# A two-layer decoder trunk on one core: the FFN output product of 22 row tiles, 14 of them as seven products of half blocks

## The chip, the cores and the metric

The kernel runs on one core of a Trainium2 chip. A core has a matrix engine (TensorE, in profiles PE for matmuls and PEld for loading their stationary operand), VectorE (DVE), ScalarE (ACT), GpSimd (POOL) and SyncE (SP, which here only issues DMAs). The metric is the device time of one execution in microseconds (us). Before the change the median of three runs is 1255.21 us (1253.51 to 1259.88).

## The reference

Two layers work on 512 tokens of 1024 features, in float32. Layer 0 mixes tokens with a convolution module, layer 1 with native sparse attention (NSA); after each mixer comes the same dense network (FFN) with its own weights. The inner width D_FF is 2816.

```python
for i in range(DEPTH):                       # DEPTH = 2
    h = rmsnorm(x, norm_mix[i])
    y = conformer_conv_module(h, ...) if i == 0 else nsa_attention(h, positions, ...)
    x = x + y
    h = rmsnorm(x, norm_ffn[i])
    x = x + swiglu_ffn(h, ffn_w_in[i], ffn_w_out[i])

def swiglu_ffn(h, w_in, w_out):
    gate, up = jnp.split(h @ w_in, 2, axis=-1)
    return (jax.nn.silu(gate) * up) @ w_out      # (512 x 2816) @ (2816 x 1024)
```

## The kernel before

All activations are kept transposed: x is eight tiles x[m] of 128 features by 512 tokens. Products run in float32 precision by splitting: each float32 operand is written as a high part (rounded to the fast format fp32r, by ScalarE) and a low part (the rest, by VectorE), and a block product is three matmuls: high x high, low x high and high x low. In the names, `wh` and `wl` are the two parts of weights, `ah` and `al` those of the FFN's inner activations y, `hh` and `hl` those of the normalized input.

**Weights.** A planned list `units` gives the order of all weight tiles of 128 x 1024 floats. SyncE loads them into a ring of three buffers `wr` (`w_dma`, line 188); `w_hi` (ScalarE, line 198) and `w_lo` (VectorE, line 207) split them into rings `wh` and `wl` of two buffers each. `next_w` takes the next unit, issues its split and loads ahead.

**Inner part of the FFN.** The 22 row tiles of gate and up are 5 plain ones and 17 "pairs". A pair replaces the eight half-block products of a 2 x 2 scheme by seven (Strassen's way), on sums of weights and of activations: 84 matmuls with 256 columns (`product`, line 840). The weight sums of a pair come from GpSimd: `s_pre` loads a tile S (line 803), `s_acc` adds a second block to it by an accumulating DMA (line 807), and `s_add` forms two further sums (lines 814 and 815). They are split like weights (`s_part`, lines 823 and 824).

**Output part.** For each output tile m the 22 row tiles are used plainly, in units of 8, 8 and 6 blocks: a block is three matmuls of 512 columns (`mm3`, lines 258 to 260), so a layer has 22 x 8 x 3 = 528. `OUT_ORDER` interleaves the first two m, since the activations are only just being made. When a tile m is complete, VectorE adds it to x (line 985) and, in layer 0, `finish_x` prepares the next stage: the split of x (ScalarE, and VectorE in line 293) and the sum of its squares (`sum_x`: the addition in line 302 is GpSimd's for all tiles but the last, by `fin`). The same happens at the end of the convolution module and of NSA. In layer 1 the result is stored instead, the last tile in two halves of 256 columns.

**Rope tables.** `rope_tables` (lines 995 to 1018) computes sine and cosine tables for NSA, thirteen operations on VectorE and three on ScalarE, and is called within layer 0's output part.

**Order.** Within the inner part and the output part most instructions are kept in the order in which the program writes them on each engine (`pe`, `held`, `parted`); elsewhere a scheduler chooses.

Of the kernel before, what the change touches and what calls it, by code (L numbers as in the profile page):

```python
# [91 lines left out]
OUT_ORDER = [(m, b) for b in range(3) for m in range(2)] + [(m, b) for m in range(2, NK) for b in range(3)]  # L92
OUT_N = 256
# [15 lines left out]
def trunk(ctx: ExitStack, tc: tile.TileContext, A, out):  # L109
# [27 lines left out]

    def add_ffn(l):
# [5 lines left out]
        for m, b in OUT_ORDER:  # L144
            add("fw_o8", l * 16 + m * 2 + b, 1024) if b < 2 else add("fw_o6", l * 8 + m, 768)
# [37 lines left out]
    def w_dma(i):  # L183
        if i in raws or i >= len(units):
            return
        ap, cols = units[i]
        t = wp.tile([P, 1024], F32, tag="wr", name=f"wr{i}")
        raw_dma[i] = after(nc.sync.dma_start(t[:, :cols], ap), state.get("behind"))
        raws[i] = t
# [98 lines left out]
    def split_x(m, gcol):  # L288
# [3 lines left out]
        nc.scalar.activation(hh[m], x[m], AF.Copy, scale=g)  # L292
        nc.vector.scalar_tensor_tensor(hl[m], x[m], g, hh[m], ALU.mult, ALU.subtract)

    def sum_x(m, acc, eng=None, on_v=False):
        sq = acc if m == 0 else tp.tile([P, T], F32, tag="sq", name=nm("sq"))
        if on_v:
            nc.vector.tensor_tensor(sq, x[m], x[m], ALU.mult)
        else:
            nc.scalar.activation(sq, x[m], AF.Square)  # L300
        if m > 0:
            (eng or nc.gpsimd).tensor_tensor(acc, acc, sq, ALU.add)  # L302
# [4 lines left out]

    def fin(m):
        return nc.vector if m == NK - 1 else nc.gpsimd
# [57 lines left out]
    def proj_tile(pool, tag, xh=None, xl=None, mid=None, fixed=False):  # L367
# [16 lines left out]
        return ps  # L384


    def conv_module():
        acc = new_acc()
        with ExitStack() as cx:
# [307 lines left out]
            acc = new_acc()  # L697
            for m in range(NK):
# [6 lines left out]
    def ffn(acc, gnext, layer, between=None):  # L705
# [9 lines left out]
        with ExitStack() as cx:  # L715
# [3 lines left out]
            pa = cx.enter_context(tc.tile_pool(name="fpa", bufs=2, space=PSUM, reuse_waits="tile"))  # L719
            sx = ExitStack()  # L720
# [78 lines left out]

            def s_pre(n):  # L800
                if n < NST:
                    S[n] = sw.tile([P, 2 * T], F32, tag="S", bufs=3, name=nm("S"))
                    pe(nc.gpsimd.dma_start(S[n], fw_x(n)[:, :2 * T]))

            def s_acc(n):
                if n < NST:
                    pe(nc.gpsimd.dma_start(S[n].rearrange("p (a b) -> p a b", a=2),  # L807
                                           fw_x(n)[:, None, 2 * T:].to_broadcast([P, 2, T]), accum_op=ALU.add))

# [57 lines left out]
            def pair(n, prev):  # L867
# [6 lines left out]
                s_g2(n)  # L874
                s_acc(n + 2)
                s_add(n + 1)
# [55 lines left out]
            pss, w, ws = {0: bank()}, {0: next_w(False)}, {}  # L932

            def out_mm(m, fs):
                wh, wl = w[m]
                for f in fs:
                    c = slice(f % 8 * P, (f % 8 + 1) * P)
                    mm3(pss[m], wh[:, c], wl[:, c], ah[f], al[f], f == 0, f == NF - 1)

            def parts(*fs):  # L940
                for f in fs:
                    divide(f, fo)

            hold[0] = True
            out_mm(0, range(4))
            w_hi(state["next"])
            w_lo()
# [4 lines left out]
            parts(4, 5, 6, 7)  # L952
            pss[1] = bank()
            w[1] = next_w(False)
            out_mm(1, range(4))
            out_mm(0, range(4, 8))
            parts(8, 9, 10, 11)
            w_hi(state["next"])
            w_lo()
            out_mm(1, range(4, 8))  # L960
            parts(12, 13, 14, 15)
            w[0] = next_w(False)
            w_hi(state["next"])
            out_mm(0, range(8, 16))
            w_lo()
            parts(16, 17, 18)
            w[1] = next_w(False)
            w_hi(state["next"])
            out_mm(1, range(8, 16))
            w_lo()  # L970
            parts(19, 20, 21)
            hold[0] = False
            acc = new_acc() if gnext is not None else None
            for m, b in OUT_ORDER[4:]:
                if m not in pss:
                    pss[m] = bank()
                ps = pss[m]
                w[m] = next_w()
                if (m, b) == (3, 0) and layer == 0:
                    between()  # L980
                out_mm(m, range(8 * b, min(8 * b + 8, NF)))
                if b < 2:
                    continue
                if gnext is not None:
                    nc.vector.tensor_tensor(x[m], x[m], ps, ALU.add)
                    finish_x(m, gnext, acc, fin(m))
                else:
                    n = OUT_N if m == NK - 1 else T
                    for c in range(0, T, n):
                        nc.vector.tensor_tensor(x[m][:, c:c + n], x[m][:, c:c + n], ps[:, c:c + n], ALU.add)  # L990
                        nc.sync.dma_start(out[m][:, c:c + n], x[m][:, c:c + n])
# [3 lines left out]
    def rope_tables():  # L995
        rp = hx[0].enter_context(tc.tile_pool(name="rp", bufs=1))
        cosT = rp.tile([P, T], F32, name="cosT")
        sinT = rp.tile([P, T], F32, name="sinT")
        pos = tp.tile([P, T], I32, tag="sq", name="pos")
# [834 lines left out]
```

## Time and profile before

| | |
|---|---|
| median of three runs | 1255.21 us (1253.51 to 1259.88) |
| the profiled execution | 1256.96 us, span 1255.2 us, granted TensorE clock 0.995 |
| TensorE matmuls | 8015 recorded, busy 98% of the span |
| VectorE, ScalarE, GpSimd | busy 66%, 45% and 27% |
| DMA | 161.62 MB moved, 129 GB/s in the mean |
| output part of a layer | 422.7 to 547.8 us (layer 0), 1125.9 to about 1251 us (layer 1) |

The span is the time from the first to the last instruction on the profiled core; the rest of an execution lies around it. A busy share is a mean over all stages. A matmul's printed duration is longer than the distance to the next one's start, because matmuls overlap in the pipeline; what a stream costs is read from the starts. Lines "L258" name lines of the kernel.

### The profile page before, as it was taken

Reading aid. Unit: us, or ns where it says so; the run is one execution under the profiler, and the core shown is the slowest. Engines: PE = TensorE matmul, PEld = TensorE weight load, DVE = VectorE, ACT = ScalarE, POOL = GpSimd, SP = SyncE. Lnnn points to the kernel's source line nnn. Section 1 sums busy time; section 2 is a strip of 40 time slices with the busy share of each in tenths; the row PEclk is TensorE's granted clock in tenths of the full one; section 3 lists DMA queues with packets and bytes.
Section 4 is the critical chain, followed back from the end, with each engine's and each line's share of the span. In section 5 each row is a group of like instructions: output and inputs, shape, how many; then the busy total and the mean of one; then the engine's idle time right before and its main releaser. Section 6 shows DMA issues by size and latency. Waiting matters only on the chain.

```text
span 1255.2 us, 20744 instructions
## 1 busy us (share of the span) xinstructions
PE 1226.4 (98%) x8015; PEld 1036.0 (83%) x8015; DVE 827.4 (66%) x1455; ACT 566.0 (45%) x1046; POOL 340.8 (27%) x395
## 2 busy tenths in 40 slices
PE   9999899999999999999998999999999999999998
PEld 6787788799999988887777776667878999998886
DVE  6995587788888735336697777753497766656221
ACT  5221464445554533223453677773354555544111
POOL 2010021144444001132332465651303444410000
PEclk9999999999999999999998999999999999999999
DMA  8757636457766233253166011001624877722331
GB/s 304 267 133 270 170 101 185 118 148 180 185 177 161 60 110 99 93 151 112 60 150 162 18 25 36 1 18 52 197 88 112 205 192 188 181 82 97 110 112 43
DMA packets 82115, 161.62 MB, mean 129 GB/s; under 512 B 36064, under 2 KB 36960, under 8 KB 80480
## 3 DMA queue, kind: packets, MB, share of 16 engines
q1 hardware_dynamic: 65808, 108.54, 28.3%
q0 software_dynamic: 16208, 51.75, 16.2%
q8 instruction: 63, 1.03, 0.3%
q14 instruction: 36, 0.29, 0.1%
HBM read 146.73 MB, written 5.28 MB: 121 GB/s over the span
## 4 chain that ended last, share of the span: by engine, by line
PE 72%; DVE 9%; issue 9%; POOL 5%; ACT 3%; DMA 1%; SPq 1%; DVEq 0%; POOLq 0%; ACTq 0%
PE st L840 17%; PE pp L258 7%; PE pp L260 7%; PE pp L259 7%; PE st L260 7%; PE st L258 7%; PE st L259 7%; PE O L1576 3%; PE cpe L496 2%; POOL S L815 1%; POOL S L814 1%; PE T L1550 1%; DVE Pm L1522 1%; PE S L1519 1%; POOL S L807 1%
## 5 line engine op out<-in xcount | busy, mean ns | idle before, releaser
L198 ACT ACTIVATE wh<-wr 128x1024 fp32r<-128x1024 f32 (+3 forms) x158 | 160.4, 1015 | 299.1 <-PE st L259 143.3
L207 DVE TENSOR_TENSOR wl<-wr,wh 128x1024 fp32r<-128x1024 f32 (+3 forms) x158 | 191.0, 1209 | 123.6 <-ACT wh L198 123.2
L840 PE MATMUL st<-bh,sh 128*128 128x256 f32 x680 | 194.1, 285 | 0.7 <-DVE t L865 0.7
L840 PE MATMUL st<-bh,sl 128*128 128x256 f32 x680 | 192.5, 283 | 1.1 <-DVE sl L824 1.1
L840 PE MATMUL st<-bl,sh 128*128 128x256 f32 x680 | 192.0, 282 | 0.0
L258 PE MATMUL pp<-hh,wh 128*128 128x512 f32 x400 | 158.8, 399 | 2.6 <-ACT wh L198 2.4
L260 PE MATMUL pp<-hh,wl 128*128 128x512 f32 x400 | 157.4, 396 | 1.7 <-DVE wl L207 1.7
L259 PE MATMUL pp<-hl,wh 128*128 128x512 f32 x400 | 157.9, 396 | 0.0
L824 DVE TENSOR_TENSOR sl<-S,sh 128x512 fp32r<-128x512 f32 x136 | 117.4, 899 | 46.9 <-ACT sh L823 45.4
L260 PE MATMUL st<-ah,wl 128*128 128x512 f32 x352 | 139.6, 396 | 0.0
L258 PE MATMUL st<-ah,wh 128*128 128x512 f32 x352 | 139.5, 396 | 0.0
L259 PE MATMUL st<-al,wh 128*128 128x512 f32 x352 | 139.5, 396 | 0.0
L840 PEld LDWEIGHTS st<-bh,sh 128*128 128x128 f32 x680 | 129.9, 191 | 2.5 <-DVE t L865 1.1
L840 PEld LDWEIGHTS st<-bh,sl 128*128 128x128 f32 x680 | 130.1, 191 | 1.5 <-DVE sl L824 1.5
L840 PEld LDWEIGHTS st<-bl,sh 128*128 128x128 f32 x680 | 130.5, 192 | 0.1
L1537 POOL TENSOR_SCALAR Pm<-Pm,sm,gates 128x512 f32<-128x512 f32 (+3 forms) x128 | 79.8, 636 | 64.9 <-DVE sm L1533 52.2
L258 PEld LDWEIGHTS pp<-hh,wh 128*128 128x128 f32 x400 | 75.3, 188 | 23.9 <-ACT wh L198 5.0
L302 POOL TENSOR_TENSOR acc<-acc,sq 128x512 f32<-128x512 f32 x18 | 30.9, 1718 | 226.8 <-ACT sq L300 208.9
L260 PEld LDWEIGHTS pp<-hh,wl 128*128 128x128 f32 x400 | 75.2, 188 | 20.4 <-DVE wl L207 3.3
L814 POOL TENSOR_TENSOR S<-S,wr 128x512 f32<-128x512 f32 x34 | 53.9, 1586 | 135.1 <-DMA wr<-fw_in 72.9
L259 PEld LDWEIGHTS pp<-hl,wh 128*128 128x128 f32 x400 | 75.4, 188 | 18.2 <-issue 1.1
L1523 ACT ACTIVATE Pm<-Pm,mx 128x512 f32<-128x512 f32 (+3 forms) x128 | 71.0, 557 | 37.7 <-DVE mx L1522 33.2
(292 smaller groups left out, 2556.1 us busy)
## 6 DMA issues: line engine op xcount, KB each, us to landing
S<-fw_x POOLq DMA_DIRECT2D x68, 512.0 KB, 6.0
wr<-fw_in SPq DMA_DIRECT2D x46, 512.0 KB
wr<-fw_o SPq DMA_DIRECT2D x32, 512.0 KB
bd<-bands POOLq DMA_DIRECT2D x12, 1280.0 KB, 12.3
r<-fw_x SPq DMA_DIRECT2D x34, 256.0 KB
wr<-cw_in SPq DMA_DIRECT2D x14, 512.0 KB
wr<-fw_o SPq DMA_DIRECT2D x16, 384.0 KB
wr<-fw_s SPq DMA_DIRECT2D x8, 512.0 KB
```

The lines of the kernel that those rows point to most:

```text
L198: parted(after(nc.scalar.activation(hi[:, :cols], raws[i][:, :cols], AF.Copy), pin.get(AF)))
L207: parted(after(nc.vector.tensor_tensor(lo[:, :cols], raws[i][:, :cols], hi[:, :cols], ALU.subtract), pin.get(ALU)))
L258: held(nc.tensor.matmul(ps, wh, xh, start=first, stop=False))
L259: held(nc.tensor.matmul(ps, wh, xl, start=False, stop=False))
L260: held(nc.tensor.matmul(ps, wl, xh, start=False, stop=last))
L302: (eng or nc.gpsimd).tensor_tensor(acc, acc, sq, ALU.add)
L814: pe(nc.gpsimd.tensor_tensor(t[:, :T], S[n][:, :T], w[:, :T], ALU.add))
L824: pe(nc.vector.tensor_tensor(l_[:, c], z, h_[:, c], ALU.subtract))
L840: pe(nc.tensor.matmul(ps[:, :H], p_[:, k], m_[c][:, t], start=first and c == 0 and q == 0, stop=last and c == 3 and q == 2, skip_group_che ...
L1523: at_[AF] = nc.scalar.activation(Pt, Pt, AF.Exp, bias=mx, scale=-1.0, accum_out=sm)
L1537: nc.gpsimd.tensor_scalar(Pt, Pt, sm[:, k:k + 1], gates[:, t + k, br * 16 + h:br * 16 + h + 1], ALU.mult, ALU.mult)
L1576: pe(nc.tensor.matmul(o[par * 64:par * 64 + 64, P * kc:], vf[br][:, kc, g], Us[par][kc], start=False, stop=last))
```

## The change

The output part uses the first 8 row tiles (EARLY + LATE) plainly, as before, in eight units `PLAIN` of eight blocks. The other 14 are taken as 2 halves of NO = 7 row tiles; together with 2 halves of the outputs (m 0 to 3 and 4 to 7) and 2 halves of the tokens they form a 2 x 2 scheme whose eight products are replaced by seven, numbered p = 1 to 7 and done in the order `OUT_SEQ`. Each has 28 blocks (4 outputs x 7 row tiles) of three matmuls with 256 columns: 84 matmuls, in units (p, u) of 8, 8, 8 and 4 blocks. The plain units stand between them as slots P1 to P7 (`PLAIN_AT`). In layer terms 528 matmuls of 512 columns become 192 of 512 and 588 of 256; PE's instruction list grows by 504 rows.

For p = 1, 4 and 7 the weights are quarters of the matrix that come through the `wr` ring. For p = 2, 3, 5 and 6 they are sums: SyncE loads a quarter (`s_base`), GpSimd adds others by accumulating DMAs (`s_more`). One sum tile per unit is kept and carried on from product 2 to 3 to 5; the first one lies in the three S buffers of the inner part (pool `so`), the sum for p = 6 (`S6`) has its own buffers and is begun in product 4. Sums are split into the same `wh` and `wl` rings (`split_sum`). Activations need sums and differences too (`z_new`, `z_on`, on VectorE), split by `direct` and `summed`. Results of a product collect in PSUM and are added to x by `out_add`, in halves of 256 columns.

In each slot the program writes, in this order: the split of the next slot's weights, this slot's matmuls, the additions to x of the previous slot's results, and what `todo` lists for this slot.

Further edits: in a pair GpSimd's `s_add` for the next pair now stands ahead of `s_acc`; the sums of squares of the convolution's, layer 0's and NSA's outputs are added on VectorE throughout; the rope tables are computed in the convolution's output part, written to DRAM and reloaded in NSA; layer 1's last tile adds and stores one half at the end.

```diff
-OUT_ORDER = [(m, b) for b in range(3) for m in range(2)] + [(m, b) for m in range(2, NK) for b in range(3)]
+LATE = 4
+NO = (NF - EARLY - LATE) // 2
+QCOLS = 4 * NO * P
+QU = (QCOLS + 1023) // 1024
+OUT_SEQ = (1, 4, 2, 3, 5, 6, 7)
+OUT_RAW = {1: 0, 4: 1, 7: 3}
+OUT_SUMS = ((2, 3, (2,)), (3, 3, (2, 0)), (5, 3, (2, 0, 1)), (6, 0, (2,)))
...
+PLAIN_AT = {(4, 1): 3, (2, 2): 4, (3, 0): 5, (5, 0): 6, (5, 2): 7}
...
-    def fin(m):
-        return nc.vector if m == NK - 1 else nc.gpsimd
...
-                finish_x(m, V_NF0, acc, fin(m))
+                finish_x(m, V_NF0, acc, nc.vector)
+                for _ in range(3 if m > 2 else 0):
+                    if tables:
+                        tables.pop(0)()
...
+            def s_base(k, u, eng=None):
+                p, q_, _ = OUT_SUMS[k]
+                n = "S6" if p == 6 else "S"
+                if k == 0 and u < 3:
+                    sums[n, u] = so.tile([P, 2 * T], F32, tag="S", bufs=3, name=nm("So"))
+                else:
+                    sums[n, u] = fo.tile([P, ucols(u)], F32, tag=f"{n}{u}", name=nm("So"))
+                pe((eng or nc.sync).dma_start(sums[n, u], quarter(layer, q_, u)[0]))
+
+            def s_more(k, u):
+                p, _, qs = OUT_SUMS[k]
+                pe(nc.gpsimd.dma_start(sums["S6" if p == 6 else "S", u], quarter(layer, qs[-1], u)[0], accum_op=ALU.add))
...
                 s_g2(n)
+                s_add(n + 1)
                 s_acc(n + 2)
-                s_add(n + 1)
                 s_load(n + 2)
                 s_pre(n + 3)
...
+            def direct(p, g, key, h, t, sign=1.0):
+                h_, l_ = piece(key, g, p)
+                for k, i in enumerate(PAIRS[g]):
+                    c = slice(k * H, (k + 1) * H)
+                    z = half(h, i, t)
+                    pe(nc.scalar.activation(h_[:, c], z, AF.Copy, scale=sign))
...
+                        pe(nc.vector.tensor_tensor(l_[:, c], z, h_[:, c], ALU.subtract))
...
+            def split_sum(p, u):
+                n = ucols(u)
+                z = sums["S6" if p == 6 else "S", u]
+                hi = wp.tile([P, 1024], F32R, tag="wh", name=nm("soh"), bufs=2)
+                lo = wp.tile([P, 1024], F32R, tag="wl", name=nm("sol"), bufs=2)
+                pe(nc.scalar.activation(hi[:, :n], z, AF.Copy))
+                pe(nc.vector.tensor_tensor(lo[:, :n], z, hi[:, :n], ALU.subtract))
+                return hi, lo
...
+            def products(p, u, w):
+                wh, wl = w
+                done = []
+                for k in range(ucols(u) // P):
+                    j, i = divmod(8 * u + k, NO)
+                    ps = target(p, j)
+                    h_, l_ = opnd[p, i // 2]
+                    t = slice(i % 2 * H, (i % 2 + 1) * H)
+                    c = slice(k * P, (k + 1) * P)
+                    for r, (a, b) in enumerate(((wh, h_), (wh, l_), (wl, h_))):
+                        pe(nc.tensor.matmul(ps, a[:, c], b[:, t], start=p in (1, 4) and i == 0 and r == 0,
+                                            stop=i == NO - 1 and r == 2, skip_group_check=True))
...
+            def out_add(p, j):
+                dm, t, sign = ADDS[p]
+                m = j + dm
+                xs = x[m][:, t * H:(t + 1) * H]
+                pe(nc.vector.tensor_tensor(xs, xs, target(p, j), ALU.add if sign > 0 else ALU.subtract))
...
+            for u in range(QU):
+                at((2, u), L(s_more, 1, u))
+                at((3, u), L(s_more, 2, u))
+                at((4, u), L(s_base, 3, u))
+                at(((3, 3), (5, 0), (5, 1), (5, 2))[u], L(s_more, 3, u))
...
+            for n, (p, u) in enumerate(slots):
+                w = ready if p in OUT_NEW else next_w(False)
+                if n + 1 < len(slots):
+                    p1, u1 = slots[n + 1]
+                    if p1 in OUT_NEW:
+                        ready = split_sum(p1, u1)
+                    else:
+                        split_next()
...
+                sums_ = behind[:]
+                behind.clear()
+                if p == "P":
+                    plain(w, PLAIN[u])
+                    behind.extend(lambda m=m: keep_plain(m) for m, f in PLAIN[u] if f == EARLY + LATE - 1)
+                else:
+                    for j in products(p, u, w):
+                        behind.append(lambda p=p, j=j: out_add(p, j))
...
+                for f in sums_ + todo.pop((p, u), []):
+                    f()
```

The first place is PE between two units of weights, with what each matmul waits for on other engines (`st` is a bank of PSUM, `oz` an operand piece). Before, in the middle of output tile m = 2 of layer 0:

```order
L260 MATMUL st_4902<-ah_4752,wl_4905 128x512
L258 MATMUL st_4902<-ah_4786,wh_4934 128x512 [waits Activation_49]
L259 MATMUL st_4902<-al_4787,wh_4934 128x512
L260 MATMUL st_4902<-ah_4786,wl_4935 128x512 [waits DVE_49]
L258 MATMUL st_4902<-ah_4790,wh_4934 128x512
```

Now, from the end of unit (1, 3) to the start of unit (4, 0) in layer 0:

```order
L1110 MATMUL st_4933<-oz_4818,wh_4914 128x256
L1110 MATMUL st_4933<-oz_4819,wh_4914 128x256
L1110 MATMUL st_4933<-oz_4818,wl_4915 128x256
L1110 MATMUL st_4975<-oz_4856,wh_4952 128x256 [waits Activation_49]
L1110 MATMUL st_4975<-oz_4857,wh_4952 128x256
L1110 MATMUL st_4975<-oz_4856,wl_4953 128x256 [waits DVE_49]
L1110 MATMUL st_4975<-oz_4856,wh_4952 128x256
```

The first matmul of a unit still waits for the high part from ScalarE and the third for the low part from VectorE, but each matmul has half the columns, and the unit ahead here has 12 matmuls where all units before had 18 or 24.

The second place is VectorE in product 4 of layer 0 (`wl` are low parts of weights, `x_76` to `x_79` the tiles x[0] to x[3]). Before, in the same part of the program, around output tiles m = 1 and 2:

```order
L207 TENSOR_TENSOR wl_4905<-wr_4844,wh_4904 128x1024
L293 SCALAR_TENSOR_TENSOR hl_494_4896<-x_77,vec,hh_493_4895 128x512
L207 TENSOR_TENSOR wl_4935<-wr_4874,wh_4934 128x768
L207 TENSOR_TENSOR wl_4965<-wr_4907,wh_4964 128x1024
L985 TENSOR_TENSOR x_78<-x_78,st_4902 128x512
```

Now, in the slots (4, 0), (4, 1) and P3:

```order
L228 TENSOR_TENSOR wl_4972<-wr_4912,wh_4971 128x1024
L1123 TENSOR_TENSOR x_79<-x_79,st_4933 128x256
L1062 TENSOR_TENSOR oz_5003<-z_4809,oz_5002 128x512
L1062 TENSOR_TENSOR oz_5007<-z_4862,oz_5006 128x512
L228 TENSOR_TENSOR wl_5015<-wr_4950,wh_5014 128x1024
L1123 TENSOR_TENSOR x_76<-x_76,st_4975 128x256
L1080 TENSOR_TENSOR z_4809<-z_4809,y_3941 128x256
L1080 TENSOR_TENSOR z_4809<-z_4809,y_4073 128x256
L1080 TENSOR_TENSOR z_4862<-z_4862,y_4205 128x256
L1080 TENSOR_TENSOR z_4862<-z_4862,y_4337 128x256
```

Pieces of operands and additions of 256 columns now stand between the low parts, and the addition that frees the bank `st_4975` of (4, 0) stands behind the low part `wl_5015` of the next slot.

The third place is GpSimd in the inner part of layer 0, one round of the loop over pairs. Before:

```order
L803 DMA S_3486<-fw_x 128x1024
L807 DMA S_3486<-fw_x 128x2x512
L814 TENSOR_TENSOR S_318_3613<-S_3354,wr_3325 128x512
L815 TENSOR_TENSOR S_318_3613<-S_318_3613,wr_3325 128x512
L803 DMA S_3618<-fw_x 128x1024
```

Now:

```order
L877 DMA S_3778<-fw_x 128x1024
L892 TENSOR_TENSOR S_361_3904<-S_3646,wr_3617 128x512
L893 TENSOR_TENSOR S_361_3904<-S_361_3904,wr_3617 128x512
L883 DMA S_3778<-fw_x 128x2x512
L877 DMA S_3910<-fw_x 128x1024
```

Before, the accumulating load into a tile S stood right behind the plain load into it, and the additions behind it read a tile filled a round earlier. Now the additions stand ahead of the accumulating load, and they read the tile (`S_3646`) whose accumulating load was the last one issued.

More of the change, by code (lines that the diff above doesn't have):

```diff
@@ L143, in add_ffn @@
             add("fw_in", l * n + i, 1024)
-        for m, b in OUT_ORDER:
-            add("fw_o8", l * 16 + m * 2 + b, 1024) if b < 2 else add("fw_o6", l * 8 + m, 768)
+        for i in range(3):
+            add("fw_p", l * NK + i, 1024)
+        for z in OUT_SEQ:
+            for u in range(QU):
+                if z in OUT_RAW:
+                    units.append(quarter(l, OUT_RAW[z], u))
+                if (z, u) in PLAIN_AT:
+                    add("fw_p", l * NK + PLAIN_AT[z, u], 1024)
     add_ffn(0)
@@ L697, in conv_module, with table @@
             acc = new_acc()
+            follow = dict(chain)
+            def table(dt):
+                return cp.tile([P, 8, 68], dt, tag="uf", bufs=len(PE_CONV), name=nm("tab")).rearrange(
+                    "p a b -> p (a b)")[:, :T]
+            tables = list(rope_tables(table, lambda z: after(z, follow[z.ins.engine])))
             for m in range(NK):
@@ L931, in ffn, with plain, keep_plain, split_next @@
                 q = pair(n, q)
[L932 to L942, printed above, removed]
-            hold[0] = True
-            out_mm(0, range(4))
-            w_hi(state["next"])
-            w_lo()
+            hold[0] = True
+            pss, w = {}, next_w(False)
+            def plain(w, blocks, k0=0):
+                wh, wl = w
+                for k, (m, f) in enumerate(blocks, k0):
+                    if m not in pss:
+                        pss[m] = bank() if m < 3 else pa.tile([P, T], F32, tag="pa", name=nm("st"))
+                    c = slice(k * P, (k + 1) * P)
+                    mm3(pss[m], wh[:, c], wl[:, c], ah[f], al[f], f == 0, f == EARLY + LATE - 1)
+            def keep_plain(m):
+                pe(nc.vector.tensor_tensor(x[m], x[m], pss.pop(m), ALU.add))
+            def split_next():
+                w_hi(state["next"])
+                w_lo()
+            plain(w, PLAIN[0][:4])
+            split_next()
             finish(q)
@@ L965, in ffn @@
[L965 to L971, printed above, removed]
-            hold[0] = False
[L973 to L991, printed above, removed]
@@ new lines, in split_sum, with target @@
+            def split_sum(p, u):
[6 more added lines that the diff above has]
+                return hi, lo
+            AD, B = {}, {}
+            def target(p, j):
+                if p == 1 and j not in AD:
+                    AD[j] = bank()
+                if p == 4 and j not in B:
+                    B[j] = bank()
+                return B[j][:, :H] if p == 4 else AD[j][:, H:] if p in (2, 5) else AD[j][:, :H]
@@ new lines, in ffn @@
+            for p in OUT_SEQ:
+                for u in range(QU):
+                    slots.append((p, u))
+                    if (p, u) in PLAIN_AT:
+                        slots.append(("P", PLAIN_AT[p, u]))
+            acc = new_acc() if gnext is not None else None
+            plain(w, PLAIN[0][4:], 4)
+            for f in todo.pop(("P", 0)):
+                f()
+            ready = None
+            for n, (p, u) in enumerate(slots):
[4 more added lines that the diff above has]
+                        ready = split_sum(p1, u1)
+                    else:
+                        split_next()
+                elif state["next"] < state["end"]:
+                    split_next()
+                sums_ = behind[:]
[3 more added lines that the diff above has]
+                    behind.extend(lambda m=m: keep_plain(m) for m, f in PLAIN[u] if f == EARLY + LATE - 1)
+                else:
+                    for j in products(p, u, w):
+                        behind.append(lambda p=p, j=j: out_add(p, j))
+                if n + 1 == len(slots):
+                    sums_ += behind
+                for f in sums_ + todo.pop((p, u), []):
+                    f()
+                while finals:
+                    m = finals.pop(0)
+                    finish_x(m, gnext, acc, nc.vector)
@@ L1673, in trunk @@
     cx0.close()
[L1674 to L1677 removed]
+    acc = ffn(acc, V_NM1, 0)
+    acc = nsa(acc, V_NF1)
     ffn(acc, None, 1)
```

187 lines of the change are left out of this document (131 added, 56 removed).

## The prediction

> **What bounds the kernel now.** I read the page first: span, busy shares, and the chain that ended last.
>
> ```profile
> span 1255.2 us, 20744 instructions
> PE 1226.4 (98%) x8015; PEld 1036.0 (83%) x8015; DVE 827.4 (66%) x1455; ACT 566.0 (45%) x1046; POOL 340.8 (27%) x395
> PE 72%; DVE 9%; issue 9%; POOL 5%; ACT 3%; DMA 1%; SPq 1%; DVEq 0%; POOLq 0%; ACTq 0%
> ```
>
> TensorE is busy 98% of the span and carries 72% of the chain. The averages hide stages, so next come the windows of the two dense layers: inner product of layer 0, output product of layer 0, then the same of layer 1 (columns: window, length, busy time with instruction count for PE, PEld, DVE, ACT and POOL, granted clock, DMA share, GB/s).
>
> ```profile
> core 0: us, PE busy (x) PEld busy (x) DVE busy (x) ACT busy (x) POOL busy (x), PEclk, DMA share, GB/s
> 250.00:384.00 134.00, 133.16 (x1103) 131.80 (x1102) 112.00 (x144) 68.12 (x128) 60.67 (x51) 1.00 0.66 169
> 422.70:548.00 125.30, 125.30 (x543) 101.05 (x542) 55.34 (x73) 42.72 (x60) 15.58 (x15) 1.00 0.30 93
> 957.00:1090.00 133.00, 132.47 (x1112) 132.26 (x1111) 94.72 (x148) 70.50 (x133) 59.99 (x54) 1.00 0.70 180
> 1126.00:1250.00 124.00, 124.00 (x537) 99.97 (x536) 43.04 (x52) 31.66 (x41) 0.00 (x0) 1.00 0.28 92
> ```
>
> In both output products (second and fourth row) PE never idles, at full clock, while VectorE is busy 35 to 44% and DMA moves 92 to 93 GB/s. So a matmul taken out there shortens the kernel, as long as VectorE, ScalarE and DMA can feed what replaces it. The timeline gives what a matmul costs there, and what one with 256 columns costs in the inner part's half-block products.
>
> ```profile
> 540.07 0.39 PE L258 MATMUL st<-ah,wh 128*128 128x512 f32 x1
> ...
> 547.10 0.40 PE L258 MATMUL st<-ah,wh 128*128 128x512 f32 x1
> ```
>
> ```profile
> 389.61 0.28 PE L840 MATMUL st<-bl,sh 128*128 128x256 f32 x1
> ...
> 392.24 0.28 PE L840 MATMUL st<-bh,sl 128*128 128x256 f32 x1
> ```
>
> The printed durations overlap; what counts is the pitch from start to start. Thirty steps lie between the first two rows: 7.03/30 = 0.2343 us. Twenty-two lie between the other two: 2.63/22 = 0.1195 us; I take 0.119. Half the columns, half the pitch.
>
> By the Trainium skill, "TensorE: Matmul & The Clock Gate", section "Back-to-back issue gap", the spacing in a stream is set by weight load and matmul together, about 131 ns at 512 columns and 81 ns at 128, so halving the columns would save far less than half; an estimate by interpolation puts 256 columns at 98 ns, three quarters of the 512 figure, and at that ratio the change would cost some 24 us a layer. The rows above differ from it (234 and 119 ns, ratio 1.97), so the measurement decides.
>
> **PE's matmuls.** The diff replaces 528 matmuls of 512 per layer by 8 plain rows (8 × 8 × 3 = 192 of 512) and seven products of 28 blocks (7 × 28 × 3 = 588 of 256). Before: 528 × 0.2343 = 123.7 us. After: 192 × 0.2343 + 588 × 0.119 = 45.0 + 70.0 = 115.0 us. That is −8.7 us a layer, −17.4 in all, if PE never waits.
>
> **The split of the next weights, new bound.** Each unit of weights goes through a ring of two split buffers: ScalarE writes the high part, VectorE subtracts the low part, PE reads. In the output product of layer 0 one turn reads:
>
> ```profile
> 543.12 0.40 PE L259 MATMUL st<-al,wh 128*128 128x512 f32 x1
> ...
> 543.55 1.06 ACT L198 ACTIVATE wh<-wr 128x1024 fp32r<-128x1024 f32 x1 [4.73 <-PE st L259]
> ...
> 544.64 1.23 DVE L207 TENSOR_TENSOR wl<-wr,wh 128x1024 fp32r<-128x1024 f32 x1 [4.84 <-ACT wh L198]
> ```
>
> The matmul at 543.12 is the last reader of its buffer (0.40 long); then 1.06 for the high part, 0.03 gap, 1.23 for the low part, ending at 545.87. The split can start when the unit before last is read out, so about when the previous unit begins. Counted from there: 0.07 + 1.06 + 0.03 + 1.22 + 0.05 = 2.43 us until a matmul can read the low part; it is the third matmul of its unit. A unit of 24 matmuls of 512 lasts 5.62 us, so before the change this is covered more than twice. A unit of 24 matmuls of 256 lasts 24 × 0.119 = 2.86 us: covered by 0.4. But 28 blocks are cut 8 + 8 + 8 + 4, and the last unit of each product lasts 12 × 0.119 = 1.43 us. The third matmul of the unit after it would be due at 1.43 + 2 × 0.119 = 1.67 and can read at 2.43: a wait of 0.76. What PE loses beside the wait itself shows in the one such stall of the inner part:
>
> ```profile
> 957.80 0.28 PE L840 MATMUL st<-bl,sh 128*128 128x256 f32 x1
> 957.87 1.89 DVE L824 TENSOR_TENSOR sl<-S,sh 128x512 fp32r<-128x512 f32 x3
> ...
> 958.61 0.39 PE L840 MATMUL st<-bh,sl 128*128 128x256 f32 x1 [0.53 <-DVE sl L824]
> ...
> 958.84 0.28 PE L840 MATMUL st<-bh,sh 128*128 128x256 f32 x1
> ```
>
> The first matmul after the wait takes 0.23 to the next instead of 0.12, so a stall costs 0.11 more: 0.87 in all. Six products end in a half unit with another full unit behind them (the seventh is the end): 6 × 0.87 = 5.2 us a layer.
>
> Two further places. In slot (1,0) VectorE has, behind the low part, two additions of 512 columns and six pieces of 256; per piece I use these rows:
>
> ```profile
> 386.94 0.42 DVE L857 TENSOR_TENSOR y<-st,g 128x256 f32<-128x256 f32 x1
> 387.28 0.42 DVE L858 TENSOR_TENSOR y<-t,g 128x256 f32<-128x256 f32 x1
> ...
> 1131.02 4.90 DVE L742 TENSOR_TENSOR al<-y,ah 128x512 fp32r<-128x512 f32 x8
> ```
>
> Pitch 0.335 for 256 columns, 4.90/8 = 0.61 for 512: 1.2 + 2.0 = 3.2 us beside a low part of 1.14 in a slot of 2.86, so it falls 1.5 behind, 0.4 to 0.7 of it caught by slack: about 0.86 with the restart. In slot (4,1) the first matmul of product 4's third block of outputs reuses the bank that the addition for (4,0) frees, and that addition stands on VectorE behind the low part for the plain unit that follows: about 0.74. Sum of waits per layer 5.2 + 0.9 + 0.7 = 6.8. Layer 0 also prepares the next stage (ScalarE copies, VectorE subtractions and square sums for each finished x tile, now on VectorE instead of GpSimd) inside the same slots: +1.9, from 8 × 0.61 more on VectorE, of which less than half falls on a slot without slack. Out stage: 2 × (−8.7 + 6.8) + 1.9 = −1.9 us. The bounds: nothing of this stalls (−17.4); each of some 28 transitions stalls the 0.87 (24 − 17 = +7 a layer, +14).
>
> **Inner loop on GpSimd.** The order in a pair becomes: the two additions, then the accumulating DMA, then the next plain load. Before, GpSimd waits for the plain load ahead of the accumulating one:
>
> ```profile
> 264.15 1.18 POOL L807 DMA_DIRECT2D S<-fw_x  x1 [5.58 <-DMA S<-fw_x]
> 264.89 1.75 POOL L814 TENSOR_TENSOR S<-S,wr 128x512 f32<-128x512 f32 x1
> 266.72 1.65 POOL L815 TENSOR_TENSOR S<-S,wr 128x512 f32<-128x512 f32 x1
> 268.31 0.61 POOL L803 DMA_DIRECT2D S<-fw_x  x1
> 274.97 1.18 POOL L807 DMA_DIRECT2D S<-fw_x  x1 [6.05 <-DMA S<-fw_x]
> ...
> 1025.35 1.18 POOL L807 DMA_DIRECT2D S<-fw_x  x1 [3.75 <-DMA S<-fw_x]
> ```
>
> In layer 0 the loop takes 274.97 − 264.15 = 10.8 us against 84 × 0.119 = 10.0 on PE, so GpSimd sets the pace there; in layer 1 the wait is 3.75 and the period PE's 10.0. The landing times by line:
>
> ```profile
> L807 POOL DMA_DIRECT2D S<-fw_x x34: 1170/1180/1242, 195.4 to 1095.4; - x34
> ...
> DMA to landing us min/median/max: 5.7/6.2/8.6
> ```
>
> After, a plain load has a whole period to land and leaves the loop; what remains is accumulating load plus additions: 6.2 + (1.75 + 1.65) = 9.6, with bounds 5.7 + 2.65 = 8.4 and 8.6 + 3.4 = 12.0. What layer 0 loses stands in the windows above: 1103 matmuls in 134.00 us, where layer 1 runs 1112 in 133.00; at layer 1's rate 1103 take 131.9. So −2, bounds −3 (the whole 173 us of the part at that ratio) and +5 a layer.
>
> The Trainium skill, "SBUF — State Buffer", section "SBUF: two separate sides", warns that a DMA issued from GpSimd can starve for descriptors while VectorE holds the port that they share. The L807 row holds 1170 to 1242 ns through stages where VectorE is busy 112.0 of 134.0 us, which does not show it.
>
> **Transfers.** The output product now moves per layer 8 plain tiles, 10.5 raw half-block tiles and 21 for the four weight sums (loads and accumulations, of which the first sum's lie in the inner part's end), 512 KB each. Without the 7 of the first sum that is 32.5 × 0.524 = 17.0 MB in 115 to 122 us, 140 to 148 GB/s against 93 before and 169 to 180 in the inner part. The mean is covered by what the inner part already sustains. The accumulations are issued a product ahead, ten or more us before use, against the 8.6 of the slowest landing. The tight stretch is product 4: its four raw units, a plain one and the S6 loads share SP's queue. I take +0.6, bounds 0 and +4.
>
> **The rest.** The rope tables and square sums move into the convolution's output; there GpSimd's adds and VectorE's splits stretch each other:
>
> ```profile
> 172.67 5.88 DVE L293 SCALAR_TENSOR_TENSOR hl<-x,vec,hh 128x512 fp32r<-128x512 f32 x4
> ...
> 173.28 4.72 POOL L302 TENSOR_TENSOR acc<-acc,sq 128x512 f32<-128x512 f32 x3 [65.32 <-ACT sq L300]
> ...
> 180.21 0.74 DVE L293 SCALAR_TENSOR_TENSOR hl<-x,vec,hh 128x512 fp32r<-128x512 f32 x1
> ```
>
> Four splits take 5.88/4 = 1.47 each beside GpSimd's adds, 0.74 without them. With the adds on VectorE (0.61 each) that stretch goes, so they cost about nothing; 13 rope operations of 512 columns add 8 us to VectorE behind a PE that works through the matmuls: +0.3, bounds −0.5 and +2. Reloading the tables is two loads of 256 KB long before use: 0. The end:
>
> ```profile
> 1251.17 0.75 DVE L990 TENSOR_TENSOR x<-x,st 128x256 f32<-128x256 f32 x2 [8.24 <-PE st L260]
> ```
>
> Two additions of 256 before, one after: −0.3.
>
> **Sum.** −1.9 − 2.0 + 0.6 + 0.3 − 0.3 = −3.3. The profiled execution took 1256.96 (span 1255.2 plus 1.76 around it), so 1253.7; it stood 1.75 above the median of 1255.21, so I predict 1252.
>
> **Rivals.** (A) *The splits keep up.* If a wait at a half unit is absorbed, because ScalarE or VectorE start earlier than I count, the whole −17.4 arrives: 1255.2 − 17.4 − 1.4 = 1236.5. For it: both engines are under half busy there. Against it: the ring has two buffers and the chain of 2.43 is longer than 1.67 whatever else is idle. Chance 0.17; partly so (half the waits gone, 1245) is inside the forecast's tail.
> (B) *The transfers of product 4 are late*, slower than before. Four raw units (3.5 tiles), the plain one and at least one S6 load, 5.5 tiles or 2.9 MB, are needed within 13 us: 222 GB/s. Below that rate PE waits; at 169 it takes 17.1 us, +4 a layer, and the last product's 3.5 tiles within 10 us (183 GB/s) add 0.8; with later units paying the same again in the ring, +5 to +8 a layer: about 1265. For it: no window above holds over 180. Against it: none of them asked for more. Chance 0.14.
> (C) *GpSimd's loop gets longer*: if accumulating loads land at 7.0 in the mean and the additions take 3.4, the period is 10.4 and 15 periods in two layers give +12 less the 2 counted: 1266. It decides from a landing of 6.6. Chance 0.09.
>
> **How the numbers follow.** The forecast, waits at the half units eating most of the gain, has 0.55, with its own range 1246 to 1258; 0.05 is left for what I do not see. No change means within 0.5%, 6.3 us, about what a measurement here can tell: 1249 to 1261.5. Faster takes A (0.17) and the forecast's lower fifth (0.11) with a little of the rest: 0.30; slower takes B and C nearly whole: 0.21; the same 0.49. The range reaches to A's and to B's side: 1239 to 1264.
>
> **What would show it.** Right: in the output product PE waits of about 0.8 us at the third matmul of the unit after each half unit, ended by the low part of the split on VectorE, six a layer, and none at the other units; about 588 matmuls of 256 at 0.119 each; a period of 10.0 in layer 0's inner loop. Wrong: PE without idle time there (A), waits for a high part that itself waits for a load (B), a longer period with GpSimd waiting for the accumulating load (C), or waits at full units too, which would mean that the small operations on VectorE and ScalarE, not the ring, set the pace.

## The result, and the profile after

The changed kernel takes 1270.55 us (median of four runs, 1267.65 to 1276.4) against 1256.85 for the kernel before beside it: a ratio of 1.0119, 95% interval 1.0084 to 1.0154. I had predicted 1252 and a range up to 1264; it is slower by 1.2%. The page of the profile after:

```profile
span 1269.3 us, 22103 instructions
PE 1217.7 (96%) x8519; PEld 1046.3 (82%) x8519; DVE 900.5 (71%) x1654; ACT 603.5 (48%) x1116; POOL 346.6 (27%) x417
```

TensorE is busy 8.7 us less than before, and the span is 14.1 us longer. The windows of the two inner parts and the two output parts tell where. First the kernel before, from the first matmul of a part to the first of the next, or, in layer 1's output part, to about the end of its last matmul (inner and output part of layer 0, then of layer 1; columns as in the prediction):

```profile
249.90:422.70 172.80, 171.56 (x1418) 169.60 (x1417) 141.15 (x185) 88.18 (x166) 72.14 (x60) 1.00 0.62 161
422.70:547.80 125.10, 125.10 (x543) 100.86 (x541) 55.33 (x72) 42.52 (x60) 15.38 (x15) 1.00 0.30 92
956.26:1125.85 169.59, 169.06 (x1417) 168.85 (x1416) 116.70 (x185) 89.36 (x166) 68.07 (x60) 1.00 0.63 164
1125.85:1250.97 125.12, 125.12 (x542) 100.69 (x540) 43.04 (x52) 31.66 (x41) 0.00 (x0) 1.00 0.28 91
```

Then the changed kernel, where the output part of layer 0 also ends with its own last matmul, since the first one of NSA comes 0.9 us later (553.32):

```profile
249.10:429.34 180.24, 174.32 (x1417) 169.96 (x1416) 126.22 (x185) 89.40 (x166) 74.88 (x64) 1.00 0.65 166
429.34:552.40 123.06, 118.21 (x794) 107.40 (x792) 86.53 (x152) 56.95 (x89) 19.58 (x31) 1.00 0.62 154
960.63:1143.47 182.84, 175.54 (x1417) 170.19 (x1416) 126.14 (x185) 89.26 (x166) 75.12 (x65) 1.00 0.64 163
1143.47:1266.10 122.63, 117.95 (x794) 107.38 (x792) 80.62 (x143) 49.72 (x76) 13.23 (x16) 1.00 0.62 156
```

The output parts got shorter by 2.0 and 2.5 us; 0.9 of the 2.0 is lost again in that wait at the start of NSA. The inner parts, with the same matmuls, got longer by 7.4 and 13.2. So the loss lies in the part whose loop differs in the place of one line: GpSimd's additions ahead of the accumulating load. Its timeline in layer 1, one round after the change:

```profile
976.39 1.30 POOL L892 TENSOR_TENSOR S<-S,wr 128x512 f32<-128x512 f32 x1 [5.92 <-DVE sl L902]
977.77 1.63 POOL L893 TENSOR_TENSOR S<-S,wr 128x512 f32<-128x512 f32 x1
979.34 1.19 POOL L883 DMA_DIRECT2D S<-fw_x  x1
980.10 1.02 POOL L877 DMA_DIRECT2D S<-fw_x  x1
987.47 1.29 POOL L892 TENSOR_TENSOR S<-S,wr 128x512 f32<-128x512 f32 x1 [6.35 <-issue]
```

and SyncE's queue in the same stretch, where L209 is the load of raw weights:

```profile
975.86 0.33 SPq L854 DMA_DIRECT2D r<-fw_x  x1
979.42 0.33 SPq L209 DMA_DIRECT2D wr<-fw_in  x1
```

From the accumulating load (979.34) to the next additions, which read its result, pass 8.13 us; the additions and the gap to the next accumulating load take 2.95 (976.39 to 979.34). The round is 11.08 us, TensorE's 84 matmuls 10.0. Over the pairs of both layers the first of the two is 7.85 us in the median, and a round takes 10.8 us in the mean in layer 0 and 11.0 in layer 1. The raw load starts 0.08 us after the accumulating one: it goes into the buffer of raw weights that the additions have just read, so their end releases both (SyncE's waits for L209 end with L893). In the kernel before, in layer 1, the same operations stand apart:

```profile
982.86 0.61 POOL L803 DMA_DIRECT2D S<-fw_x  x1
987.61 1.18 POOL L807 DMA_DIRECT2D S<-fw_x  x1 [4.14 <-DMA S<-fw_x]
```

```profile
983.92 0.38 SPq L188 DMA_DIRECT2D wr<-fw_in  x1
```

There the raw load starts 1.1 us behind the plain load into S and 3.7 us ahead of the accumulating load.

What the raw load does to the accumulating one shows in the data that the two queues move after the issue at 979.34 (q1 carries SyncE's loads, q0 GpSimd's). The first pair of lines is the stretch from 980.40 to 982.20, the second from 982.20 to 985.50:

```profile
DMA packets 108, 0.43 MB, mean 241 GB/s; under 512 B 2, under 2 KB 2, under 8 KB 108
q1 hardware_dynamic: 108, 0.43, 90.0%
...
q0 software_dynamic: 269, 0.57, 97.9%
q1 hardware_dynamic: 33, 0.08, 6.4%
```

The raw load, issued 0.08 us later, moves its data first, and in that time GpSimd's queue moves nothing. Over the pairs of both layers the accumulating load's data begin 3.2 us after its issue; in e1 below, where no raw load stands beside it, 2.0 us.

The landing times of the accumulating load after the change (minimum, median, maximum; 5.7, 6.2 and 8.6 before):

```profile
L883 POOL DMA_DIRECT2D S<-fw_x x34: 1173/1192/1247, 197.3 to 1122.6; - x34
...
DMA to landing us min/median/max: 6.2/7.6/11.0
```

What TensorE waits for, by the list of waits (total, times, longest), is an operation on VectorE in the inner part (L943; I read it as the last link of that chain, and e1 bears it out), and the splits and one addition in the output part:

```profile
PE st L918 <- DVE t L943: 11.6, 15, 1.2
...
PE st L1110 <- DVE sol L1088: 4.7, 8, 0.7
...
PE st L1110 <- DVE wl L228: 3.7, 6, 0.7
...
PE st L1110 <- DVE x L1123: 1.0, 2, 0.5
```

### The profile page after: what moved, and what is told of

It is laid out like the page before. It is cut to its first block, busy times and chain, and to the rows that moved or that the text cites. A ratio compares the mean times of both kernels' runs of the same rounds, so it can differ in the third digit from the quotient of the medians.

```text
span 1269.3 us, 22103 instructions
## 1 busy us (share of the span) xinstructions
PE 1217.7 (96%) x8519; PEld 1046.3 (82%) x8519; DVE 900.5 (71%) x1654; ACT 603.5 (48%) x1116; POOL 346.6 (27%) x417
## 5 line engine op out<-in xcount | busy, mean ns | idle before, releaser
L219 ACT ACTIVATE wh<-wr 128x1024 fp32r<-128x1024 f32 (+3 forms) x150 | 152.4, 1017 | 192.9 <-PE pp L280 60.8
L228 DVE TENSOR_TENSOR wl<-wr,wh 128x1024 fp32r<-128x1024 f32 (+3 forms) x150 | 181.6, 1211 | 43.7 <-ACT wh L219 43.3
L918 PE MATMUL st<-bh,sh 128*128 128x256 f32 x680 | 197.7, 291 | 12.2 <-DVE t L943 11.6
L902 DVE TENSOR_TENSOR sl<-S,sh 128x512 fp32r<-128x512 f32 x136 | 134.3, 1012 | 101.9 <-ACT sh L901 95.4
L892 POOL TENSOR_TENSOR S<-S,wr 128x512 f32<-128x512 f32 x34 | 46.5, 1368 | 337.7 <-issue 156.7
L901 ACT ACTIVATE sh<-S 128x512 fp32r<-128x512 f32 x136 | 81.2, 623 | 56.2 <-DMA S<-fw_x 34.0
L1110 PE MATMUL st<-oz,soh 128*128 128x256 f32 x448 | 80.0, 280 | 0.0
L1715 DVE CUSTOM_DVE_ANT_0 Pm<-S,mask 128x512 f32<-128x512 f32 (+3 forms) x128 | 59.1, 483 | 28.0 <-PE S L1713 27.5
L918 PE MATMUL st<-bl,wh 128*128 128x256 f32 x272 | 76.2, 280 | 0.0
```

The source lines that it names most:

```text
L219: parted(after(nc.scalar.activation(hi[:, :cols], raws[i][:, :cols], AF.Copy), pin.get(AF)))
L228: parted(after(nc.vector.tensor_tensor(lo[:, :cols], raws[i][:, :cols], hi[:, :cols], ALU.subtract), pin.get(ALU)))
L901: pe(nc.scalar.activation(h_[:, c], z, AF.Copy))
L902: pe(nc.vector.tensor_tensor(l_[:, c], z, h_[:, c], ALU.subtract))
L918: pe(nc.tensor.matmul(ps[:, :H], p_[:, k], m_[c][:, t], start=first and c == 0 and q == 0, stop=last and c == 3 and q == 2, skip_group_che ...
L1110: pe(nc.tensor.matmul(ps, a[:, c], b[:, t], start=p in (1, 4) and i == 0 and r == 0, stop=i == NO - 1 and r == 2, skip_group_check=True))
```

## The experiments

All times beside the kernel before are from runs on the same chip; stage lengths come from each kernel's profile, as in the windows above.

**e1, the order put back.**

```diff
-                s_add(n + 1)
                 s_acc(n + 2)
+                s_add(n + 1)
```

> The changed kernel with GpSimd's order in a pair put back (accumulating load, additions, plain load); all else as changed. Theory 1 (the plain load, issued 0.75 us behind the accumulating one, shares the transfer with it, so that both land after about 8 us and the loop of accumulating load and additions grows to 11 us): the inner parts return from 180.2 and 182.8 us to about 172.8 and 169.6, the total falls by about 20 us to 1250. Theory 2 (something else in the change lengthens the inner part, such as the new place of the S buffers): inner parts stay above 178 us each, total about 1270.

Measured: 1249.2 us against 1252.45, ratio 0.9961 (0.9941 to 0.9980). The inner parts:

```profile
249.16:418.74 169.58, 169.04 (x1417) 168.84 (x1416) 118.51 (x185) 89.27 (x166) 71.58 (x66) 1.00 0.69 179
...
952.23:1121.81 169.58, 169.05 (x1418) 168.84 (x1417) 117.19 (x185) 89.38 (x166) 71.53 (x66) 1.00 0.69 179
```

Both take TensorE's own time, and the output parts are unchanged (123.9 with NSA's first wait, where the changed kernel has 124.0, and 122.6). One line carries the whole loss; without it the change is a small gain. This refutes theory 2.

**e2, the new order alone in the kernel before.**

```diff
-                s_acc(n + 2)
                 s_add(n + 1)
+                s_acc(n + 2)
```

> The kernel before with only GpSimd's order in a pair changed (additions, accumulating load, plain load). Theory 1: inner parts of 180 and 183 us, total 1257 + 20 = 1277, the accumulating loads' median landing 7.6 instead of 6.2 us. Theory 2: no change, 1257, within 3 us.

Measured: 1283.29 us, ratio 1.0231 (1.0200 to 1.0263), inner parts 185.9 and 186.2 us, accumulating loads landing in 8.1 us (median), the raw load 0.1 us behind them again. The loss comes with the order of these lines, without the rest of the change; the price is 3 to 6 us a layer above that in the changed kernel, and why was not settled.

**e3, the plain load on the other queue.**

```diff
-                    pe(nc.gpsimd.dma_start(S[n], fw_x(n)[:, :2 * T]))
+                    pe(nc.sync.dma_start(S[n], fw_x(n)[:, :2 * T]))
```

> The changed kernel, with its order on GpSimd, but the plain load into S issued by SyncE on the hardware queue. Theory 1a (the two loads hold each other up because they share GpSimd's queue): accumulating loads land in about 6.2 us again, the period is 10.0, inner parts about 170 each, total about 1249. Theory 1b (they share the DMA engines and the path to memory, whichever queue): accumulating loads still land in 7 to 8 us, inner parts 176 to 183, total 1262 to 1271.

Measured: 1272.89 us, ratio 1.0157 (1.0122 to 1.0191), inner parts 185.9 and 182.1, landing 8.0. It refutes 1a: the plain load now starts 4.5 us ahead of the accumulating one, and nothing is gained. In its timeline the raw load is what still starts with the accumulating load (984.47 and 984.40 us). That left the question which load is the partner, and the next two each take one away.

**e5, the plain load cut to an eighth.**

```diff
-                    S[n] = so.tile([P, 2 * T], F32, tag="S", bufs=3, name=nm("S"))
-                    pe(nc.gpsimd.dma_start(S[n], fw_x(n)[:, :2 * T]))
+                    S[n] = so.tile([P, 2 * T], F32, tag="S", bufs=3, name=nm("S")) if n < 3 else S[n - 3]
+                    c = 2 * T if n < 3 else P
+                    pe(nc.gpsimd.dma_start(S[n][:, :c], fw_x(n)[:, :c]))
```

> The changed kernel with its order on GpSimd; from the fourth pair on the plain load into S brings only 128 of its 1024 columns (the rest of the tile keeps what it had, so the sums of weights are wrong). Theory 1b (three transfers of 512 KB, the accumulating load, the plain load and the next raw weights, start together when the additions end, and the accumulating one gets a third of the path): with one of the three gone it lands in about 7 us instead of 8, the period falls from 11.0 to 10.0 to 10.3, inner parts 170 to 174. Theory 3 (the loop of accumulating load and additions is too long by itself, without any sharing): accumulating load still 7.6 to 8, inner parts 180 to 183.

**e8, the raw load cut to an eighth.**

```diff
...
-        t = wp.tile([P, 1024], F32, tag="wr", name=f"wr{i}")
+        small = i in few and i - 3 in few
+        t = raws[i - 3] if small else wp.tile([P, 1024], F32, tag="wr", name=f"wr{i}")
+        ap, cols = (ap[:, :P], P) if small else (ap, cols)
```

> The changed kernel with its order on GpSimd; in 12 of the 17 pairs of a layer the raw weights come with 128 of their 1024 columns (the rest of the buffer keeps what it had, so these weights are wrong). Theory 1b: as with the plain load cut, the accumulating load lands in about 7 us in these pairs, and their period falls to 10.0 to 10.3. Theory 1c (only loads of GpSimd's own hold each other up): no change, period 11.0 in these pairs.

Both kernels leave out data that the result needs, so they serve only to time the loop. Measured (one run each, so the inner parts are compared and not the totals): e5 1271.81 us, inner parts 180.4 and 183.8; e8 1250.59 us, inner parts 170.0 and 169.6. The landing of the accumulating load in e5:

```profile
L884 POOL DMA_DIRECT2D S<-fw_x x34: 1174/1186/1247, 196.2 to 1122.7; - x34
DMA to landing us min/median/max: 6.3/7.9/9.4
```

and in e8:

```profile
L887 POOL DMA_DIRECT2D S<-fw_x x34: 1163/1192/1247, 196.3 to 1101.4; - x34
DMA to landing us min/median/max: 5.8/6.9/9.0
```

I had expected an even share among three loads, and got something else. With 448 of 512 KB of the plain load gone the accumulating load is no faster; with the raw load cut it lands 0.7 us sooner than in the changed kernel (7.6), its data begin 2.0 us after the issue again, and the whole stall is gone. The small plain load itself, 64 KB, still takes 7.3 us to land in e5, nearly as long as the full one (8.4), so it waits behind the accumulating load in their common queue. The partner is the raw load on SyncE's queue. In e8 it also starts 1.3 us ahead of the accumulating load, because only the first addition reads the columns that it still fills; and the additions with the gap behind them take 2.6 us there instead of 2.95, which is part of what the round gains. e5 alone would have fitted theory 3, too; e8 refutes it, since the same loop fits into 10 us there.

**e9, the raw load in GpSimd's queue,** with nothing left out:

```diff
...
-        raw_dma[i] = parted(after(nc.sync.dma_start(t[:, :cols], ap), state.get("behind")))
+        if i in few:
+            raw_dma[i] = tc.keep_in_program_order(nc.gpsimd.dma_start(t[:, :cols], ap))
+        else:
+            raw_dma[i] = parted(after(nc.sync.dma_start(t[:, :cols], ap), state.get("behind")))
```

> The changed kernel with its order on GpSimd; from the fifth pair on, the raw weights are loaded by GpSimd behind the plain load, so that all three loads stand in one queue; nothing is left out. Theory 4 (loads of one queue go one after the other, and what slows the accumulating load is the raw load on the other queue): the accumulating load lands in 6.0 to 6.4 us, the period is 10.0, inner parts 170 to 172, total about 1249. Rival (any 512 KB under way at the same time slows it, whichever queue): 7.5 to 8 us, inner parts 180 to 183, total about 1270.

Measured: 1247.11 us against 1252.72, ratio 0.9944 (0.9923 to 0.9964), both inner parts 169.6 us. A round of its timeline:

```profile
975.16 1.23 POOL L888 DMA_DIRECT2D S<-fw_x  x1
975.93 1.04 POOL L882 DMA_DIRECT2D S<-fw_x  x1
976.48 1.03 POOL L212 DMA_DIRECT2D wr<-fw_in  x1
982.03 1.29 POOL L897 TENSOR_TENSOR S<-S,wr 128x512 f32<-128x512 f32 x1 [4.51 <-DMA S<-fw_x]
```

All three loads start within 1.4 us, as in the changed kernel, but one behind the other, and the additions follow 6.87 us after the accumulating load instead of 8.13 (medians over both layers 7.2 and 7.85). The landing (median 6.9) missed my 6.0 to 6.4; the stage came out as expected. So the new order is not bad in itself: it costs time where the raw load stands on the other queue and gets ahead. e9 changes two things at once, the queue and the start of the raw load (1.3 us behind the accumulating load instead of 0.1); whether a later start on SyncE's queue would have been enough was not run.

**e6, the kernel before, once more.**

> The kernel before, once more with a profile. If layer 0's longer inner part (172.8 against 169.6 us in layer 1) belongs to the kernel, it shows again, 172 to 173; if it is a matter of the single execution, it lies elsewhere between 169.6 and 174.

Measured (one run): 1250.88 us, and the two inner parts:

```profile
248.65:418.25 169.60, 169.06 (x1418) 168.86 (x1417) 117.37 (x185) 89.38 (x166) 67.17 (x60) 1.00 0.63 164
950.21:1119.78 169.57, 169.03 (x1417) 168.83 (x1416) 116.21 (x185) 89.14 (x166) 67.77 (x60) 1.00 0.64 164
```

The 172.8 us of layer 0 did not come again here, but it is no single accident: with the same order on GpSimd the traces show layer 0 at 173.2 us in e10 and both layers at 171.3 and 171.9 in e7 (both below), while e1, e4 and e6 have 169.6 in both. The loop runs in one of two ways, at full clock in both. In the first (layer 0 of the kernel before) the raw load starts 0.08 us behind the plain load, which lands in 5.9 us (median), and GpSimd sets a round of 10.3 us in the mean; in the second (e6) the raw load starts 1.05 to 1.4 us behind, the plain load lands in 3.9 to 4.0, and the additions wait for VectorE. So in the old order, too, a load of GpSimd's is slower where the raw load starts right behind it. What decides which way a layer runs was not tested.

**e4, units of seven blocks,** on top of e1:

```diff
-QU = (QCOLS + 1023) // 1024
+UC = NO * P
+QU = QCOLS // UC
...
-                    j, i = divmod(8 * u + k, NO)
+                    j, i = divmod(NO * u + k, NO)
```

> As e1, and the 28 blocks of each product cut into four units of seven (896 columns) instead of 8, 8, 8 and 4. Theory of the ring (a short unit gives the next split too little time: 0.07 + 0.94 + 0.03 + 1.08 + 0.05 = 2.17 us against 21 x 0.119 + 0.24 = 2.7): the waits of about 0.6 us at the start of a unit go, each output part falls from 122.8 to about 117.5 us, total about 10 us under e1, 1240. Rival (the many small operations on VectorE and ScalarE set the pace): the waits move to other units, output parts stay at 121 to 123, total within 3 us of e1.

**e7, a third split buffer,** on top of e1, units of 8, 8, 8 and 4; every third slot's split goes to a buffer of its own:

```diff
+    third = [None]
+
+    def split_tiles():
+        p, h = (third[0], "3") if third[0] else (wp, "")
+        return [p.tile([P, 1024], F32R, tag=f"w{z}{h}", name=nm(f"w{z}"), bufs=1 if h else 2) for z in "hl"]
...
+                third[0] = fo if n % 3 == 0 else None
...
```

> As e1 (units of 8, 8, 8 and 4), with a third buffer for the high and low parts in the output part. Theory of the ring: the split of the next unit may start one unit earlier, so the half unit no longer cuts it short; the waits go as in the kernel with units of seven, output parts 117 to 119 us instead of 122.5 to 123.9, total about 10 us under e1. Rival (VectorE and ScalarE are kept by small operations): output parts stay above 121.

Measured: e4 1238.05 us against 1252.45, ratio 0.9871 (0.9846 to 0.9896); e7 1233.05 against 1255.01, ratio 0.9822 (0.9798 to 0.9847). The output parts of e4:

```profile
417.75:536.63 118.88, 116.67 (x795) 106.94 (x793) 87.46 (x154) 57.76 (x90) 17.30 (x28) 1.00 0.63 157
1110.79:1227.86 117.07, 116.14 (x793) 107.00 (x792) 80.63 (x143) 49.73 (x76) 11.19 (x13) 1.00 0.63 158
```

and of e7:

```profile
419.56:534.94 115.38, 115.38 (x795) 107.07 (x794) 88.85 (x155) 58.00 (x90) 16.36 (x22) 1.00 0.63 162
1112.26:1227.52 115.26, 115.26 (x794) 106.96 (x792) 80.63 (x143) 49.05 (x76) 12.04 (x14) 1.00 0.62 158
```

Two remedies of different kind, fitting the unit to the ring or the ring to the unit, both shorten the output parts: by 5.0 and 5.5 us in e4 against e1 (123.9 and 122.6), by 8.5 and 7.3 in e7, where PE is busy for the whole window. In e4 most of the waits at the short units are gone; three stay in layer 0 and one in layer 1, the longest (0.93) in unit (1, 2), the place that I had put down to the small operations of slot (1, 0). VectorE does the same work in all of them (80.6 us in layer 1), so what set the pace was the ring and not the amount of small operations; with the third buffer they cost PE nothing.

**e10, both remedies.**

> Units of seven and a third split buffer together (order on GpSimd as before the change). The output parts with the third buffer alone took 115.4 and 115.3 us without a wait of PE, so nothing is left there: theory of the ring: the same time as with the third buffer alone, 1233, within 4 us. Rival (the two remedies work on different waits): 1228 or less.

Measured: 1235.5 us against 1252.72, ratio 0.9845 (0.9817 to 0.9873), output parts 115.4 and 115.3: the same as e7, as expected (layer 0's inner part ran the first of the two ways named under e6). e7 and e10 are the best versions run, both faster than the kernel before and than the changed one.

## Why the prediction was wrong

**The step that failed** is the one on GpSimd's inner loop: "what remains is accumulating load plus additions: 6.2 + (1.75 + 1.65) = 9.6", and −2 for layer 0. The 6.2 was measured in an order in which the raw load started about 3 to 6 us ahead of the accumulating one. I counted what the swap moves on GpSimd and not what the end of the additions releases on SyncE's queue. In the changed kernel the two start within 0.1 us and the raw load's data go first; the accumulating load takes 7.85 us to its reader where I had 6.2, the round 10.8 and 11.0 us instead of 10.0, and the two layers pay 7.4 and 13.2 us: +20.6 where I had −2. This is rival C in its effect, to which I gave 0.09 and 1266; C did not name the raw load. Its rule, that it decides from a landing of 6.6, was somewhat low: in e8 and e9 the median was 6.9 and TensorE did not wait, because the additions with their gap took 2.6 us and not the 3.4 that I had read in layer 0 of the kernel before.

**The −2 itself** rested on one execution, and on one round of 10.8 us where the mean of that layer is 10.3. The reading that GpSimd set the pace there was right for that execution; e6 shows layer 0 at 169.6 in the unchanged kernel, so where the loop runs the second of its two ways there was nothing to gain.

**PE's matmuls** came out right: 115.0 us were worked out for a layer. With the 12 matmuls of 256 columns that still belong to the last pair (1.4), 116.4 would be due; e7, without a wait, takes 115.3 to 115.4, since the pitch is 0.117: (115.38 − 45.0)/600.

**The waits at half units** came out right in place, kind and size. In layer 0 of the changed kernel TensorE's timeline shows eight waits of 0.5 us or more, at the eight places of my sum: behind the six half units, in unit (1, 2) and in (4, 1). Four of them:

```profile
454.31 0.39 PE L1110 MATMUL st<-oz,wl 128*128 128x256 f32 x1 [0.59 <-DVE wl L228]
459.48 0.39 PE L1110 MATMUL st<-oz,wl 128*128 128x256 f32 x1 [0.63 <-DVE wl L228]
464.96 0.51 PE L1110 MATMUL st<-oz,wh 128*128 128x256 f32 x2 [0.51 <-DVE x L1123]
...
475.63 0.40 PE L1110 MATMUL st<-oz,soh 128*128 128x256 f32 x2
476.68 0.38 PE L1110 MATMUL st<-oz,sol 128*128 128x256 f32 x1 [0.65 <-DVE sol L1088]
476.90 0.39 PE L1110 MATMUL st<-oz,soh 128*128 128x256 f32 x2
```

454.31 is in (1, 2), 459.48 begins behind (1, 3), 464.96 is in (4, 1), 476.68 lies behind (4, 3). The bracket counts only idle time; the delay is read from the starts. The third matmul of the unit at 475.63 was due two pitches later, at 475.86, and started at 476.68, 0.82 late; the next came 0.22 behind it instead of 0.12, together 0.92 where I had 0.87. So read, the six behind half units sum to 5.3 us (predicted 5.2), (1, 2) is 0.87 (0.86) and (4, 1) is 0.79 (0.74). One more at a full unit, 0.4 us at 537.40, was not in my sum. Between the changed kernel and e7 the output parts differ by 123.98 − 115.38 = 8.6 us in layer 0, with the wait of NSA's first matmul, and, from first to last matmul, by 7.2 in layer 1, against 6.8 plus 1.9 and 6.8. What layer 0 pays more than layer 1 is thus 1.4 us where I had put 1.9, and most of it is that wait, not the waits inside the part. The agreement of 8.6 with 8.7 is partly luck.

The output parts gave −2.0 + 0.9 − 2.5 = −3.6 us in all, where I had −1.9. My upper bound for them was added up wrongly: 24 is what 28 stalls cost in one layer, 17 the gain of two; it should have read 24.4 − 8.7 = +15.7 a layer. The stages outside the four windows took 3.0 us less in all (without that wait), where I had +0.3 − 0.3; NSA alone differs by 1.6 us between two executions of the kernel before, so I read nothing into it.

**The transfers (rival B)** were hidden: no wait of TensorE in the output part ends in a load, and none of ScalarE's there, at 154 to 156 GB/s; my +0.6 for them did not come. **The splits keep up (rival A)** is refuted by the waits above; e7 shows what it would have brought. Without the swapped line my sum would have been −1.3; e1 measured −3.3 us by the medians (1249.2 against 1252.45) and −4.9 by the ratio (1252.45 × 0.0039).

## What to carry to other kernels

Before an order is changed on an engine off the critical path, list every buffer that its instructions release, and which load on which queue starts then: a landing time read from a trace holds only for the neighbours that the load had there. When a product is made of fewer, shorter matmuls, check each unit against the time of the split chain that runs beside it, the shortest unit first; a ring of two buffers gives a split only the length of one unit. And a gain that is read from a difference between two stages of one execution should be seen in a second one before it goes into a sum: here the same loop ran in two ways, and which one came changed from one execution to the next.

## What the runs showed of the hardware

A load issued later can go first. In the changed kernel the data of SyncE's raw load began 1.0 us after its issue, those of GpSimd's accumulating load 3.2 us after theirs, 0.1 us earlier on the clock; without such a neighbour (e1, e6) the accumulating load's data began after 2.0 us. So the raw load had the path to itself from about 1 to 3 us after the issue, and the additions read the accumulating load's result 7.85 us after its issue (median).

Loads of 512 KB in GpSimd's one queue landed one behind the other: in e9 the medians of the three, counted from the accumulating load's issue, are 6.9, 8.2 and 9.6 us. The first still lands 0.9 us later than in e1 (6.0); whether the loads behind it cost that was not tested. And a load of 64 KB behind an accumulating one took 7.3 us to land (e5), not much less than one of 512 KB in its place (8.4).
